# Instance norm over rows of 4096: batch-norm statistics on VectorE for three rows of a tile, two ScalarE passes for the fourth, both engines normalising

## The chip, the cores and the metric

One core of a Trainium2 chip. The metric is the device time of one execution in microseconds (us). The kernel before takes 4961.82 us (median of 4 runs, 4961.57 to 4962.37).

## The reference

```python
x = np.random.randn(256, 256, 4096).astype(np.float32)      # eps = 1e-5
mean = np.mean(x, axis=2, keepdims=True)
var = np.var(x, axis=2, keepdims=True)
out = ((x - mean) / np.sqrt(var + eps)).astype(np.float32)
```

That is 65,536 independent rows of 4096 float32 numbers: 1.07 GB in and 1.07 GB out. The chip's engines that matter here are VectorE (DVE in the profiles) and ScalarE (ACT), which compute, SyncE (SP), which issues the transfers, and 16 DMA engines, which carry them out. Engines wait for each other through semaphores, counters that an instruction or a transfer increments. A transfer has landed when each of the 16 DMA engines has incremented its semaphore.

## The kernel before

The rows go through 128 tiles of 128 partitions x 4 rows (8.39 MB each) in three buffers. One queue on SyncE issues everything in a fixed order, store t and then load t+2:

```python
def store(s, t):
    take(S, done[s], K + 1)              # all rows of the tile are normalised
    S.dma_start(out=rows_of(out_t, t), in_=X[s][:, :, :]).then_inc(stored[s], 16)

def load(s, t, wait=True):
    if wait:
        take(S, stored[s], 16)           # the buffer's last store has landed
    S.dma_start(out=X[s][:, :, :], in_=rows_of(x_t, t)).then_inc(loaded[s], 16)
# ...
with S.Fori(0, rounds) as i:
    for t in range(L0, L0 + BUFS):
        store(t % BUFS, (t, BUFS, rounds, i))
        load((t + 2) % BUFS, (t + 2, BUFS, rounds, i))
```

Per tile VectorE takes the sum of each row in a pass that writes the row back and accumulates, ScalarE takes the sum of squared deviations, and VectorE normalises, except for three quarters of the last row, which ScalarE does:

```python
for r in range(r0, r0 + k):
    V.tensor_scalar(out=x[:, r, :], in0=x[:, r, :], scalar1=1.0 / d, scalar2=None, op0=ALU.mult, op1=ALU.add,
                    accum_out=mean[s][:, r : r + 1]).then_inc(means, 1)
# ... ScalarE, row by row:
A.activation(out=junk, in_=x[:, r, :], func=AF.Square, bias=mean[s][:, c], scale=-float(d), accum_out=ss[s][:, c])
# ... VectorE: reciprocal, bias product, and
V.tensor_scalar(out=x[:, r, f], in0=x[:, r, f], scalar1=rstd[s][:, c], scalar2=nbias[s][:, c],
                op0=ALU.mult, op1=ALU.add).then_inc(dn, 1)
```

The first and the last tile go in halves of two rows. The whole kernel:

## Time and profile before

| | before |
|---|---|
| time, median | 4961.82 us |
| busy VectorE, ScalarE | 66%, 49% |
| busy DMA engines | 9 tenths or more in every slice, 433 GB/s |
| period of a tile | 38.64 us in most of the run |
| landing of a load to issue of the tile's store | 26.2 us |

Read it from the DMA side: 2147.5 MB have to pass, and the engines that pass them are never idle. What SyncE's queue waits for (line, who waits for whom: us in total, times, longest) doesn't contradict that:

```profile
SPq L68 <- DVE x L112: 4757.1, 130, 38.3
SPq L68 <- DMA out_dram<-x: 47.7, 3, 30.7
```

SyncE waits for VectorE nearly all the time, but SyncE only issues transfers. Those that it has issued before are still under way meanwhile. The prediction shows the lines that tell it.

### The profile page before, as it was taken

How to read it: one execution, taken by the hardware profiler on the slowest of the kernel's cores; microseconds unless marked ns; L12 is line 12 of the kernel's file. 1: busy time of each engine (PE TensorE's matmuls, PEld its weight loads, DVE VectorE, ACT ScalarE, POOL GpSimd, SP SyncE). 2: the span in 40 equal slices, each digit the busy share in tenths (PEclk: the TensorE clock that was granted, in tenths of full speed). 3: DMA queues.
4: the chain of work that ended last, by engine and by line, in shares of the span. 5: the costliest groups of instructions: out<-in, count | busy, mean ns of one | idle time of the engine just before them, and what ended most of it. 6: DMA issues, size and time to landing. Idle time of an engine off the chain costs nothing.

```text
span 4960.2 us, 5938 instructions
## 1 busy us (share of the span) xinstructions
DVE 3298.0 (66%) x2049; ACT 2407.7 (49%) x1412; POOL 0.2 (0%) x4
## 2 busy tenths in 40 slices
DVE  6666666666666666666666666666666666666666
ACT  4455444554445544455445544455444554445544
POOL 0000000000000000000000000000000000000000
DMA  9999999999999999999999999999999999999999
GB/s 422 431 435 433 431 435 433 432 437 432 432 438 432 433 437 432 433 437 432 435 435 432 436 434 431 438 433 431 438 433 432 438 432 433 438 432 433 438 432 405
DMA packets 37298, 2147.52 MB, mean 433 GB/s; under 512 B 4144, under 2 KB 4144, under 8 KB 4144
## 3 DMA queue, kind: packets, MB, share of 16 engines
q1 hardware_dynamic: 37296, 2147.50, 100.0%
q14 instruction: 2, 0.02, 0.0%
HBM read 1073.74 MB, written 1073.74 MB: 433 GB/s over the span
## 4 chain that ended last, share of the span: by engine, by line
DVE 62%; another core or an unknown queue 31%; issue 4%; DMA 2%; ACT 0%; DVEq 0%; ACTq 0%; SPq 0%
DVE x L87 44%; DVE x L112 17%; DMA x<-in_x_dram 1%; DVE nbias L100 1%; DMA out_dram<-x 1%; DVE rstd L98 1%; ACT junk L137 0%; DVEq L68 0%; DVEq L219 0%; ACT L146 0%; ACT std L146 0%; ACTq L68 0%; ACTq L67 0%; SPq L265 0%
## 5 line engine op out<-in xcount | busy, mean ns | idle before, releaser
L87 DVE TENSOR_SCALAR_CACHE_REDUCE x<-x 128x4096 f32<-128x4096 f32 x512 | 2232.3, 4416 | 1580.4 <-DMA x<-in_x_dram 1580.4
L137 ACT ACTIVATE junk<-x,mean 128x4096 f32<-128x4096 f32 x512 | 1883.1, 3678 | 2367.2 <-DVE x L87 2367.2
L112 DVE TENSOR_SCALAR x<-x,rstd,nbias 128x4096 f32<-128x4096 f32 (+1 forms) x512 | 1004.2, 2004 | 33.9 <-DVE nbias L100 29.3
L151 ACT ACTIVATE x<-x,nbias,rstd 128x3072 f32<-128x3072 f32 x130 | 383.2, 2948 | 146.2 <-DVEq L68 146.2
L137 ACT ACTIVATION_READ_ACCUMULATOR junk<-x,mean 128x1 f32 x512 | 95.5, 187 | 0.0
L146 ACT ACTIVATE std<-ss,eps_tile 128x2 f32<-128x2 f32 x256 | 75.6, 295 | 19.1
L98 DVE RECIPROCAL rstd<-std 128x2 f32<-128x2 f32 x256 | 40.7, 159 | 19.4 <-ACT std L146 19.4
L100 DVE SCALAR_TENSOR_TENSOR nbias<-mean,rstd 128x2 f32<-128x2 f32 x256 | 41.1, 161 | 8.9
L87 DVE DVE_READ_ACCUMULATOR x<-x 128x1 f32 x512 | 42.3, 83 | 0.0
L137 ACT ACT_TABLE_LOAD x1 | 1.3, 1283 | 1.2 <-DVE eps_tile L216 1.2
L146 ACT ACT_TABLE_LOAD x1 | 1.3, 1283 | 0.1
L216 DVE MEMSET eps_tile<- 128x1 f32 x1 | 0.1, 59 | 1.0 <-SPq L192 1.0
L251 POOL MEMSET const-bfloat16-1.0<- 128x1 bf16 x1 | 0.1, 101 | 0.0
L251 POOL MEMSET const-uint8-127<- 128x1 uint8 x1 | 0.1, 101 | 0.0
L251 POOL MEMSET const-float32-1.0<- 128x1 f32 x1 | 0.1, 99 | 0.0
L251 POOL MEMSET const-float32-0.0<- 128x1 f32 x1 | 0.1, 98 | 0.2 <-issue 0.2
## 6 DMA issues: line engine op xcount, KB each, us to landing
out_dram<-x SPq DMA_DIRECT2D x4, 4096.0 KB, 19.6
x<-in_x_dram SPq DMA_DIRECT2D x2, 4096.0 KB, 16.7
x<-in_x_dram SPq DMA_DIRECT2D x127, 50.3
out_dram<-x SPq DMA_DIRECT2D x126, 31.5
```

The costliest lines, as they stand in the source:

```text
L87: V.tensor_scalar(out=x[:, r, :], in0=x[:, r, :], scalar1=1.0 / d, scalar2=None, op0=ALU.mult, op1=ALU.add, accum_out=mean[s][:, r : r + 1 ...
L98: mine(V.reciprocal(out=rstd[s][:, c], in_=std[s][:, c]))
L100: mine(V.scalar_tensor_tensor(out=nbias[s][:, c], in0=mean[s][:, c], scalar=-1.0 / d, in1=rstd[s][:, c], op0=ALU.mult, op1=ALU.mult))
L112: V.tensor_scalar(out=x[:, r, f], in0=x[:, r, f], scalar1=rstd[s][:, c], scalar2=nbias[s][:, c], op0=ALU.mult, op1=ALU.add,).then_inc(dn, 1)
L137: mine(A.activation(out=junk, in_=x[:, r, :], func=AF.Square, bias=mean[s][:, c], scale=-float(d), accum_out=ss[s][:, c]))
L146: A.activation(out=std[s][:, c], in_=ss[s][:, c], func=AF.Sqrt, bias=eps_tile, scale=1.0 / d**3).then_inc(stds, 1)
L151: A.activation(out=x[:, last, :Q], in_=x[:, last, :Q], func=AF.Identity, bias=nbias[s][:, c], scale=rstd[s][:, c]).then_inc(dn, 1)
L216: V.memset(eps_tile, eps / d**2).then_inc(ready, 1)
L251: nc = _bacc.Bacc("TRN2", target_bir_lowering=False, num_devices=1)
```

## The change

The intent is to take work off VectorE. Row 0 of a tile gets its mean and its variance from two ScalarE passes; rows 1 to 3 get theirs from the batch-norm instructions, which give both in one reading pass without writing the row; ScalarE normalises rows 0 and 1 and part of row 3, VectorE row 2 and the rest. Cut to its core:

```diff
-    Q = 3072
+    Q = 2752
+    F = 512
...
-        for r in range(r0, r0 + k):
-            V.tensor_scalar(out=x[:, r, :], in0=x[:, r, :], scalar1=1.0 / d, ..., accum_out=mean[s][:, r : r + 1],
-            ).then_inc(means, 1)
+        for r in range(r0 + 1, r0 + k):
+            for j in range(d // F):
+                mine(V.bn_stats(out=stats[s][:, r, j, :], in_=x[:, r, j * F : (j + 1) * F]))
+                if j == 4 and (r - r0) % 2 == 0:
+                    scales(r - 2)
+            V.wait_ge(own_v, own)
+            V.bn_aggr(out=mv[s][:, r, :], in_=stats[s][:, r]).then_inc(means, 1)
...
-        for r in range(r0, last + 1):        # ScalarE: squares of all rows
+        A.activation(out=junk, in_=x[:, r0, :], func=AF.Identity, scale=1.0 / d, accum_out=mv[s][:, c, 0])
+        A.activation(out=junk, in_=x[:, r0, :], func=AF.Square, bias=mv[s][:, c, 0], scale=-1.0, accum_out=ss[s][:, c])
...
+            for r, f in [(b + 1, slice(0, Q))] if final else [(b, slice(0, d)), (b + 1, slice(0, d))]:
+                A.activation(out=x[:, r, f], in_=x[:, r, f], func=AF.Identity, bias=nbias[...], scale=rstd[...])
```

`mine` gives each statistics instruction an increment of a semaphore. SyncE's part is the same.

More of the change, by code (lines that the diff above doesn't have):

```diff
@@ L30 @@
     n, d = x_flat.shape
-    assert n % (P * K) == 0 and d & (d - 1) == 0
+    assert n % (P * K) == 0 and d % F == 0
     ntiles = n // (P * K)
@@ L47 @@
     X = [pool.tile([P, K, d], fp32, name=f"x{s}") for s in range(BUFS)]
-    mean, ss, std, rstd, nbias = (
-        [pool.tile([P, K], fp32, name=f"{name}{s}") for s in range(BUFS)]
-        for name in ("mean", "ss", "std", "rstd", "nbias")
+    stats = [pool.tile([P, K, d // F, 6], fp32, name=f"stats{s}") for s in range(BUFS)]
+    mv = [pool.tile([P, K, 2], fp32, name=f"mv{s}") for s in range(BUFS)]
+    ss, std, rstd, nbias = (
+        [pool.tile([P, K], fp32, name=f"{name}{s}") for s in range(BUFS)] for name in ("ss", "std", "rstd", "nbias")
     )
@@ L57 @@
     stored = [nc.alloc_semaphore(f"stored{s}") for s in range(BUFS + 1)]
+    landed = nc.alloc_semaphore("landed")
+    own_a = nc.alloc_semaphore("own_a")
     own_v = nc.alloc_semaphore("own_v")
-    own_a = nc.alloc_semaphore("own_a")
     means = nc.alloc_semaphore("means")
@@ L82, in mine, with scales @@
             return instruction.then_inc(own_v, 1)
-        if ld:
-            take(V, ld, 16)
-        for r in range(r0, r0 + k):
-            V.tensor_scalar(
-                out=x[:, r, :], in0=x[:, r, :], scalar1=1.0 / d, scalar2=None, op0=ALU.mult, op1=ALU.add,
-                accum_out=mean[s][:, r : r + 1],
-            ).then_inc(means, 1)
-        for b in range(r0, r0 + k, 2):
-            c = slice(b, b + 2)
-            final = b == r0 + k - 2
-            if final:
-                take(V, stds, (b - r0) // 2 + 1)
-            else:
-                V.wait_ge(stds, (b - r0) // 2 + 1)
+        def scales(b, final=False):
+            c = slice(b, b + 2)
+            wait = take if final else (lambda engine, sem, count: engine.wait_ge(sem, count))
+            wait(V, stds, (b - r0) // 2 + 2)
             mine(V.reciprocal(out=rstd[s][:, c], in_=std[s][:, c]))
@@ L100, in vector_tile @@
             mine(V.scalar_tensor_tensor(
-                out=nbias[s][:, c], in0=mean[s][:, c], scalar=-1.0 / d, in1=rstd[s][:, c], op0=ALU.mult, op1=ALU.mult
+                out=nbias[s][:, c], in0=mv[s][:, c, 0], scalar=-1.0, in1=rstd[s][:, c], op0=ALU.mult, op1=ALU.mult
             ))
-            if final:
-                take(V, own_v, own)
-            else:
-                V.wait_ge(own_v, own)
-            if final:
-                V.sem_inc(scaled, 1)
-            for r in range(b, b + 2):
-                c = slice(r, r + 1)
-                f = slice(Q, d) if r == r0 + k - 1 else slice(0, d)
-                V.tensor_scalar(
-                    out=x[:, r, f], in0=x[:, r, f], scalar1=rstd[s][:, c], scalar2=nbias[s][:, c],
-                    op0=ALU.mult, op1=ALU.add,
-                ).then_inc(dn, 1)
+            wait(V, own_v, own)
+            V.sem_inc(scaled, 1)
+        if ld:
+            take(V, ld, 16)
+        V.sem_inc(landed, 1)
+        for r in range(r0 + 1, r0 + k):
[5 more added lines that the diff above has]
+            V.bn_aggr(out=mv[s][:, r, :], in_=stats[s][:, r]).then_inc(means, 1)
+        scales(r0 + k - 2, final=True)
+        for r in (r0 + k - 2, r0 + k - 1):
+            c = slice(r, r + 1)
+            f = slice(Q, d) if r == r0 + k - 1 else slice(0, d)
+            V.tensor_scalar(
+                out=x[:, r, f], in0=x[:, r, f], scalar1=rstd[s][:, c], scalar2=nbias[s][:, c],
+                op0=ALU.mult, op1=ALU.add,
+            ).then_inc(dn, 1)
     def scalar_tile(s, r0=0, k=K, ld=None, dn=None):
@@ L120, in scalar_tile @@
         dn = done[s] if dn is None else dn
-        last = r0 + k - 1
-        own = 0
-        def mine(instruction):
-            nonlocal own
-            own += 1
-            return instruction.then_inc(own_a, 1)
-        for r in range(r0, last + 1):
-            c = slice(r, r + 1)
-            if own:
-                A.wait_ge(own_a, own)
-            if r == last:
-                take(A, means, k)
-            else:
-                A.wait_ge(means, r - r0 + 1)
-            mine(A.activation(
-                out=junk, in_=x[:, r, :], func=AF.Square, bias=mean[s][:, c], scale=-float(d), accum_out=ss[s][:, c]
-            ))
-            if (r - r0) % 2:
-                c = slice(r - 1, r + 1)
-                if r == last:
-                    take(A, own_a, own)
-                else:
-                    A.wait_ge(own_a, own)
-                A.activation(
-                    out=std[s][:, c], in_=ss[s][:, c], func=AF.Sqrt, bias=eps_tile, scale=1.0 / d**3
-                ).then_inc(stds, 1)
@@ L149, in scalar_tile @@
-        c = slice(last, last + 1)
-        take(A, scaled, 1)
-        A.activation(
-            out=x[:, last, :Q], in_=x[:, last, :Q], func=AF.Identity, bias=nbias[s][:, c], scale=rstd[s][:, c]
-        ).then_inc(dn, 1)
+        c = slice(r0, r0 + 1)
+        take(A, landed, 1)
+        A.activation(
+            out=junk, in_=x[:, r0, :], func=AF.Identity, scale=1.0 / d, accum_out=mv[s][:, c, 0]
+        ).then_inc(own_a, 1)
+        A.wait_ge(own_a, 1)
+        A.activation(
+            out=junk, in_=x[:, r0, :], func=AF.Square, bias=mv[s][:, c, 0], scale=-1.0, accum_out=ss[s][:, c]
+        ).then_inc(own_a, 1)
@@ new lines, in scalar_tile @@
+        take(A, own_a, 2)
+        A.activation(
+            out=std[s][:, c], in_=ss[s][:, c], func=AF.Sqrt, bias=eps_tile, scale=1.0 / d
+        ).then_inc(stds, 1)
+        for b in range(r0, r0 + k, 2):
+            final = b == r0 + k - 2
+            if final:
+                take(A, means, k - 1)
+            else:
+                A.wait_ge(means, b - r0 + 1)
+            c = slice(max(b, r0 + 1), b + 2)
+            A.activation(
+                out=std[s][:, c], in_=mv[s][:, c, 1], func=AF.Sqrt, bias=eps_tile, scale=1.0
+            ).then_inc(stds, 1)
+            take(A, scaled, 1)
+            for r, f in [(b + 1, slice(0, Q))] if final else [(b, slice(0, d)), (b + 1, slice(0, d))]:
+                c = slice(r, r + 1)
+                A.activation(
+                    out=x[:, r, f], in_=x[:, r, f], func=AF.Identity, bias=nbias[s][:, c], scale=rstd[s][:, c]
+                ).then_inc(dn, 1)
@@ L214 @@
             take(S, stored[s], 16)
-        V.memset(eps_tile, eps / d**2).then_inc(ready, 1)
+        V.memset(eps_tile, eps).then_inc(ready, 1)
         halves(vector_tile, 0, True)
```

## The prediction

> **What bounds the kernel now.** I read the views in this order: busy shares and slices of the page, the DMA queue, one tile in the timeline, the issue rows, and only then the chain that ended last, because here the chain alone misleads.
>
> From the page of the kernel before:
>
> ```profile
> span 4960.2 us, 5938 instructions
> DVE 3298.0 (66%) x2049; ACT 2407.7 (49%) x1412; POOL 0.2 (0%) x4
> DMA  9999999999999999999999999999999999999999
> GB/s 422 431 435 433 431 435 433 432 437 432 432 438 432 433 437 432 433 437 432 435 435 432 436 434 431 438 433 431 438 433 432 438 432 433 438 432 433 438 432 405
> q1 hardware_dynamic: 37296, 2147.50, 100.0%
> ```
>
> VectorE is at two thirds and ScalarE at half in every slice, so neither fills its time. The DMA row is 9 in all 40 slices, and packets of the one queue take 100.0% of the 16 engines' span. Each input byte is read once and each output byte written once: 2147.5 MB in 4960.2 us are 433 GB/s.
>
> One tile in the timeline, from one store to the next (start, duration, engine, line, operation):
>
> ```profile
> 2009.40 0.34 SPq L165 DMA_DIRECT2D out_dram<-x  x1
> 2009.98 0.35 SPq L170 DMA_DIRECT2D x<-in_x_dram  x1
> 2021.72 4.42 DVE L87 TENSOR_SCALAR_CACHE_REDUCE x<-x 128x4096 f32<-128x4096 f32 x1 [12.53 <-DMA x<-in_x_dram]
> ...
> 2044.66 3.14 DVE L112 TENSOR_SCALAR x<-x,rstd,nbias 128x4096 f32<-128x4096 f32 x2 [0.19 <-DVE nbias L100]
> ...
> 2047.95 0.34 SPq L165 DMA_DIRECT2D out_dram<-x  x1
> 2048.53 0.35 SPq L170 DMA_DIRECT2D x<-in_x_dram  x1
> 2060.39 4.42 DVE L87 TENSOR_SCALAR_CACHE_REDUCE x<-x 128x4096 f32<-128x4096 f32 x1 [12.59 <-DMA x<-in_x_dram]
> ```
>
> Tiles land at 2021.72 and 2060.39: a period of 38.67 us. Compute takes 26.2 us of it (landing at 2021.72 to the store's issue at 2047.95). Then both engines idle 12.5 us for the next load. A tile is 8.39 MB in and 8.39 MB out, 16.78 MB; over 38.67 us that is 434 GB/s, the rate of the whole page. So nothing in the period is left over for a stall of the queue.
>
> The issue rows show the same from the queue's side:
>
> ```profile
> x<-in_x_dram SPq DMA_DIRECT2D x127, 50.3
> out_dram<-x SPq DMA_DIRECT2D x126, 31.5
> ```
>
> Half the period, 19.3 us, is one transfer. When store t is issued at 2009.40, load t+1 has some 12 us to go (it lands at 2021.7). The store then lands after 12 + 19.3 = 31.3 us, and the load behind it after 12 + 19.3 + 19.3 = 50.6 us. That matches 31.5 and 50.3: transfers stand in line behind a queue that never empties. The store could come up to about 12 us later without a gap in that queue, and coming earlier wins it only a longer time in line.
>
> Now the chain:
>
> ```profile
> DVE 62%; another core or an unknown queue 31%; issue 4%; DMA 2%; ACT 0%; DVEq 0%; ACTq 0%; SPq 0%
> ```
>
> It charges 62% to VectorE, since it steps from each load's issue back to the VectorE instruction that released the store ahead of it. It doesn't see that the transfer stood in line after its release. The 31% of "unknown queue" is roughly the 12.5 us wait in each 38.7 us period. I let the slices and the landing times decide: the bound is the DMA engines.
>
> **What the Trainium skill says.** "DMA: Bandwidth & Descriptors", section "Bandwidth", under "Where 436 GB/s comes from", gives a fabric ceiling of 435.2 GB/s for the 16 ports. The trace agrees: 435 GB/s over 2021.70 to 2041.00 and 432 to 437 over neighbouring stretches. An estimate from that page: 2147.5 MB at 435.2 GB/s need 4934.5 us, so at most 26 us (0.5%) separate this kernel from the ceiling, start and end latency included. "HBM Reference"[...] says that a core streaming alone goes above its share of the memory, to about 425 GB/s; the trace shows slightly more, 433. "SBUF — State Buffer", section "SBUF: two separate sides", says that engine accesses and DMA don't contend. The trace agrees within its resolution: 437 GB/s over 2009.40 to 2021.70 with both engines idle, and 435 over the next 19.3 us with VectorE busy throughout. "VectorE: DVE Perf Modes", section "The perf-mode tier table", gives float32 tensor_scalar twice the single rate and reductions the single rate. The trace agrees: normalising 4096 elements takes 2411 ns, the pass with an accumulator 4416 ns. No section gives a time for the batch-norm instructions.
>
> **The change part by part.** The durations come from these groups, kept apart by shape (count | total us, mean ns):
>
> ```profile
> L87 DVE TENSOR_SCALAR_CACHE_REDUCE x<-x 128x4096 f32<-128x4096 f32 x512 | 2232.3, 4416 | 1580.4 <-DMA x<-in_x_dram 1580.4
> L137 ACT ACTIVATE junk<-x,mean 128x4096 f32<-128x4096 f32 x512 | 1883.1, 3678 | 2367.2 <-DVE x L87 2367.2
> L112 DVE TENSOR_SCALAR x<-x,rstd,nbias 128x4096 f32<-128x4096 f32 x382 | 910.3, 2411 | 33.9 <-DVE nbias L100 29.3
> L151 ACT ACTIVATE x<-x,nbias,rstd 128x3072 f32<-128x3072 f32 x130 | 383.2, 2948 | 146.2 <-DVEq L68 146.2
> L112 DVE TENSOR_SCALAR x<-x,rstd,nbias 128x1024 f32<-128x1024 f32 x130 | 104.9, 807 | 0.0
> ```
>
> Removed from VectorE per tile: four mean passes at 4.42 us, 17.7 us, with their accumulator reads (4 x 0.08), and two of three full normalisations (2 x 2.41). Added: 24 batch-norm statistics of 512 elements and three aggregations. I size the statistics from the mean pass, which also goes at one element per step: successive passes start 4.35 us apart, 1.06 ns per element; an eighth of that is 0.54 us, and I allow 0.07 us more for the fixed part of an instruction (the two-element operations take 0.16 us). That is 0.61 us each, 14.6 us in all; the aggregations, 48 inputs each, get 0.25 us each with their wait, 0.8 us. What stays: reciprocal and bias product twice (4 x 0.16), one full row at 2.41 us, and 1344 elements of the last row, interpolated between 807 ns at 1024 and 2411 at 4096: 0.97 us. Sum: 14.6 + 0.8 + 0.6 + 3.4 = 19.4 us a tile, 2480 us in all, near 50% where it had 66%.
>
> ScalarE loses four squares (4 x (3.68 + 0.19)) and keeps two passes of that size, 7.7 us. It has three small square roots instead of two, 0.9 us. It gains two full normalisations: 2948 ns for 3072 elements, scaled by the slope between its forms (its squares give at most 3678/4096 = 0.9 ns per element), makes about 3.8 us for 4096 and 2.7 us for 2752. Sum: 7.7 + 0.9 + 7.6 + 2.7 = 18.9 us, 2420 us in all, about 49% as before. Identity, square and root should share one table: before, the table was loaded twice in the whole run (1.28 us each), and I expect no load per tile.
>
> Latency of one tile, from landing: ScalarE's two passes and roots end at about 8.8 us; VectorE has by then done row 1 (8 x 0.61 + 0.35 = 5.2 us) and five pieces of row 2 (8.3 us), so it waits about half a microsecond for the roots, spends 0.6 us on the scales and releases ScalarE at 9.4 us. ScalarE normalises rows 0 and 1 until 17.1 us; VectorE finishes rows 2 and 3 near 16.8. Root, scales and the last normalisations take 0.4 + 0.7 + 3.3 us: done at about 21.5 us, against 26.2. The store is issued 4.7 us earlier, and the queue's backlog at that moment grows from 12.5 to about 17 us. All of the gain lies beside the transfers; on the path that sets the end it is worth 0.
>
> Ends: the DMA engines are the limit there too. In the kernel before the first store half is issued at 31.54 us, while load 1 still occupies the queue to about 41; the last one at 4941.7, while the store ahead of it has work to about 4949. Both come earlier by some 5 to 8 us after the change and wait that much longer. I give the ends 0 us, with 2 or 3 us of doubt either way for engines among the 16 that run ahead of others.
>
> Predicted: 4961.5 us.
>
> **The rivals.** First, compute counts: if the chain's 62% were right, 4.7 us less per tile would bring 128 x 4.7 = 600 us, so 4360 us. It would need 493 GB/s, above anything sustained in this trace; the 12.5 us idle in each period speak against it as well. Second, the batch-norm instruction is far slower than one element per step: with the other VectorE work near 4.8 us and ScalarE hidden, it becomes the bound once 24 of them exceed 38.7 - 4.8 = 33.9 us, or 1.41 us each, 2.3 times my size. At 1.5 us each the period would be near 41 us and the time about 5240 us. Nothing in the trace shows the instruction, so this can't be excluded, but even double its size stays hidden. Third, the handshakes between the two engines or a table load per use: two loads per tile would add 2.6 us and the chain would end near 24 us, still below 38.7, so 4961 us. Fourth, less engine traffic lets the DMA go faster: the 437 against 435 above would be 0.5% at the very most, and the stretches differ as much by load and store phase; a time of 4945 us would be its upper hope.
>
> **Range and chances.** The three runs before lie within 0.6 us, and every rival I believe in leaves the queue full. I take 4956 to 4966 us, mostly for small differences at the ends and in how loads and stores interleave. Faster by over 2% needs the DMA above its ceiling: 0.01. Slower by over 2% needs the second rival: 0.02. Within 2%: 0.97.
>
> **What would show it.** Right: DMA row 9 throughout and 433 GB/s; period of landings near 38.67 us; VectorE near 50%; store issued about 21 to 22 us after landing; time from issue to landing up by the 4.7 us of earlier issue, from 31.5 to about 36 us for stores and from 50.3 to about 55 for loads; VectorE idle before its tile's first statistics up from 12.5 to about 17 us. Wrong: any gap in the DMA slices, statistics of over 1.4 us, a table load in every tile, or a period that follows the compute.

## The result

The changed kernel takes 4981.48 us (median of 4 runs, 4978.88 to 4984.67), 19.7 us more than before. The ratio is 1.004 with a 95% interval of 1.0022 to 1.0057; it is the mean time of one kernel's runs over that of the other's of the same rounds, so not quite the ratio of the medians. It is slower, clear of noise, and outside the predicted range of 4956 to 4966 us.

The page of the changed kernel, the lines that answer to those shown of before:

```profile
span 4982.9 us, 7979 instructions
DVE 2480.7 (50%) x4211; ACT 2368.6 (48%) x1290; POOL 0.2 (0%) x4
DMA  9999999999999999999999999999999999999998
GB/s 421 435 430 437 432 431 437 430 436 433 435 435 433 435 431 437 434 433 435 432 436 433 435 434 430 429 435 430 429 429 429 430 433 430 430 429 430 429 433 384
q1 hardware_dynamic: 37296, 2147.50, 99.9%
x<-in_x_dram SPq DMA_DIRECT2D x127, 56.3
out_dram<-x SPq DMA_DIRECT2D x126, 37.5
```

VectorE fell from 66% to 50%, as worked out. The DMA row is still all nines but for the last slice. But its rate goes down in the course of the run, from about 434 to 430 GB/s in the last sixteen slices (the very last apart, in which the run ends): the queue is never empty and yet slower. Transfers stand in line longer (37.5 us from issue to landing of a store, 31.5 before), as stores come earlier.

The groups by shape, for the sizes that the prediction estimated (count | total us, mean ns):

```profile
L103 DVE BATCH_NORM_STATS2 stats<-x 128x6 f32<-128x512 f32 x3056 | 1846.8, 674 | 2332.9 <-DMA x<-in_x_dram 2314.4
L147 ACT ACTIVATE x<-x,nbias,rstd 128x4096 f32<-128x4096 f32 x252 | 944.1, 3793 | 71.9 <-DVEq L96 71.9
L147 ACT ACTIVATE x<-x,nbias,rstd 128x2752 f32<-128x2752 f32 x130 | 348.5, 2681 | 92.7 <-DVEq L70 92.7
L112 DVE TENSOR_SCALAR x<-x,rstd,nbias 128x1344 f32<-128x1344 f32 x130 | 126.7, 975 | 0.0
L107 DVE BATCH_NORM_AGGREGATE mv<-stats 128x2 f32<-128x48 f32 x382 | 142.0, 372 | 13.2
```

None of these is on the path. A tile's first statistics begin when its load has landed, so their starts give the period. From the timeline, three stretches of the run:

```profile
940.20 4.85 DVE L103 BATCH_NORM_STATS2 stats<-x 128x6 f32<-128x512 f32 x8 [18.90 <-DMA x<-in_x_dram]
978.87 4.85 DVE L103 BATCH_NORM_STATS2 stats<-x 128x6 f32<-128x512 f32 x8 [18.18 <-DMA x<-in_x_dram]
...
2025.06 4.85 DVE L103 BATCH_NORM_STATS2 stats<-x 128x6 f32<-128x512 f32 x8 [18.32 <-DMA x<-in_x_dram]
...
2045.71 0.34 SPq L161 DMA_DIRECT2D out_dram<-x  x1
2046.29 0.35 SPq L166 DMA_DIRECT2D x<-in_x_dram  x1
...
2063.89 4.85 DVE L103 BATCH_NORM_STATS2 stats<-x 128x6 f32<-128x512 f32 x8 [18.33 <-DMA x<-in_x_dram]
...
4047.23 4.84 DVE L103 BATCH_NORM_STATS2 stats<-x 128x6 f32<-128x512 f32 x8 [18.60 <-DMA x<-in_x_dram]
4086.12 4.85 DVE L103 BATCH_NORM_STATS2 stats<-x 128x6 f32<-128x512 f32 x8 [18.39 <-DMA x<-in_x_dram]
```

The period is 38.67 us near 940, 38.83 near 2025, 38.89 near 4047. The store is issued 20.65 us after the landing (2025.06 to 2045.71), when the load under way has 18.2 us to go. Nothing waits for compute: VectorE idles 18 us ahead of every tile.

**Where the 22.7 us between the two profiled spans arise.** The trace holds the time of each of the 16 semaphore increments by which a transfer reports its landing, one from each DMA engine. Counting tiles from 0, the last increment of the same load came at (us):

```
tile     before    changed   difference   period before / changed since the line above
 32      1248.8     1249.2       0.4
 72      2794.3     2801.4       7.1      38.64 / 38.81
120      4649.3     4670.3      21.0      38.65 / 38.94
```

Until tile 32 both are equal. From about 1400 us on the changed kernel's period is 38.82 to 38.83 us, and from about 3100 us it is near 38.95 us. So the loss has two stages, of 0.19 and of 0.31 us per tile.

**The 16 engines one by one.** The same increments say how far the first engine is ahead of the last. Before, this lead grows to 7.5 us by 1250 us and stays there until about 4490 us. In the changed kernel it is 8.0 us at 1400 us, then grows by 0.19 us per tile, to 16.2 us near 3100 us, and stays about there. Growth means that the last engine is slower than the first; that it is one engine alone, the packets show. The trace also has a start and a duration for each DMA packet: each transfer is, on each engine, eight packets of 64 KB and a small one that reports the landing. It doesn't name the engine, but each packet starts 3 or 4 ns before the one ahead of it ends, so that the packets can be strung together, engine by engine. An undisturbed 64 KB packet takes 2418 ns. Beyond that, in ns, for two successive transfers (a store, the load behind it) near 2370 us of the changed kernel:

```
                       store: excess of its 8 packets       load: excess of its 8 packets
last engine            14 14 14 47 14 23 14 28              0 0 3 1 1 1 8 1
15th engine             0  0  0  0  0  0  0  0              0 0 0 0 0 0 0 0
first engine            0  0  0  0  0  0  0  0              0 0 0 0 0 0 0 0
```

One engine of 16 loses 168 ns on each store and 15 ns on each load, 0.18 us per tile; the others lose nothing. A load counts as landed when its last engine is through, so this one engine sets the pace. Averages over 16 engines hide it. In the kernel before there is such an engine too, with 0.03 to 0.07 us on each store; it was not the last until about 4490 us, and from then to the end the period was 38.72 us.

The 38.64 us of the kernel before are no accident either: an undisturbed engine starts its 64 KB packets 2.414 us apart, and the 16 of a load and a store take 38.62 us, to which the two small packets come.

### The profile page after: what moved, and what is told of

Same layout as the page of the kernel before. It is cut to its first block, busy times and chain, and to the rows that moved or that the text cites. A ratio compares the mean times of both kernels' runs of the same rounds, so it can differ in the third digit from the quotient of the medians.

```text
span 4982.9 us, 7979 instructions
## 1 busy us (share of the span) xinstructions
DVE 2480.7 (50%) x4211; ACT 2368.6 (48%) x1290; POOL 0.2 (0%) x4
## 4 chain that ended last, share of the span: by engine, by line
another core or an unknown queue 45%; ACT 40%; DVE 9%; issue 3%; DMA 1%; DVEq 1%; ACTq 0%; SPq 0%
ACT x L147 19%; ACT junk L127 10%; ACT junk L123 10%; DVE x L112 7%; ACT std L141 1%; DMA x<-in_x_dram 1%; DVE nbias L92 1%; DVE rstd L90 1%; ACT std L131 1%; DVEq L70 0%; ACTq L70 0%; DVEq L96 0%; DVE stats L103 0%; DVEq L215 0%
## 5 line engine op out<-in xcount | busy, mean ns | idle before, releaser
L103 DVE BATCH_NORM_STATS2 stats<-x 128x6 f32<-128x512 f32 x3056 | 1846.8, 674 | 2332.9 <-DMA x<-in_x_dram 2314.4
L123 ACT ACTIVATE junk<-x 128x4096 f32<-128x4096 f32 x130 | 466.4, 3587 | 2381.2 <-DVEq L70 2381.2
L147 ACT ACTIVATE x<-x,nbias,rstd 128x4096 f32<-128x4096 f32 (+1 forms) x382 | 1292.6, 3415 | 164.6 <-DVEq L70 92.7
L127 ACT ACTIVATE junk<-x,mv 128x4096 f32<-128x4096 f32 x130 | 478.1, 3678 | 4.2
L112 DVE TENSOR_SCALAR x<-x,rstd,nbias 128x4096 f32<-128x4096 f32 (+1 forms) x260 | 429.3, 1693 | 24.3 <-DVE nbias L92 24.3
L107 DVE BATCH_NORM_AGGREGATE mv<-stats 128x2 f32<-128x48 f32 x382 | 142.0, 372 | 13.2
L141 ACT ACTIVATE std<-mv,eps_tile 128x1 f32<-128x1 f32 (+1 forms) x256 | 73.4, 287 | 0.0
L92 DVE SCALAR_TENSOR_TENSOR nbias<-mv,rstd 128x2 f32<-128x2 f32 x256 | 41.2, 161 | 8.7
L131 ACT ACTIVATE std<-ss,eps_tile 128x1 f32<-128x1 f32 x130 | 38.2, 294 | 15.0
L127 ACT ACTIVATION_READ_ACCUMULATOR junk<-x,mv 128x1 f32 x130 | 24.3, 187 | 0.0
## 6 DMA issues: line engine op xcount, KB each, us to landing
x<-in_x_dram SPq DMA_DIRECT2D x127, 56.3
out_dram<-x SPq DMA_DIRECT2D x126, 37.5
```

The source lines that it names most:

```text
L92: mine(V.scalar_tensor_tensor(out=nbias[s][:, c], in0=mv[s][:, c, 0], scalar=-1.0, in1=rstd[s][:, c], op0=ALU.mult, op1=ALU.mult))
L103: mine(V.bn_stats(out=stats[s][:, r, j, :], in_=x[:, r, j * F : (j + 1) * F]))
L107: V.bn_aggr(out=mv[s][:, r, :], in_=stats[s][:, r]).then_inc(means, 1)
L123: A.activation(out=junk, in_=x[:, r0, :], func=AF.Identity, scale=1.0 / d, accum_out=mv[s][:, c, 0]).then_inc(own_a, 1)
L127: A.activation(out=junk, in_=x[:, r0, :], func=AF.Square, bias=mv[s][:, c, 0], scale=-1.0, accum_out=ss[s][:, c]).then_inc(own_a, 1)
L131: A.activation(out=std[s][:, c], in_=ss[s][:, c], func=AF.Sqrt, bias=eps_tile, scale=1.0 / d).then_inc(stds, 1)
```

## The experiments

Two theories at first. LEAD: earlier stores let the fast engines run further ahead, until they run dry, start together, and disturb one another. For it spoke that from 3100 us on, where the lead stops growing, packets of the other engines become longer too. COUNT: the engine that loses time loses it to something that the compute engines emit per instruction; per tile the changed kernel has 43 instructions on them (4211 + 1290 in 128 tiles) where the kernel before has 27. Every kernel was run four times (run 11 five times), beside the kernel before on the same chip, whose medians then were 4962.1 to 4962.6 us.

**1. The changed kernel with late stores.** One more VectorE pass in each tile, result unchanged:

```diff
+        r = r0 + k - 1
+        mine(V.tensor_scalar(out=x[:, r, :], in0=x[:, r, :], scalar1=1.0, scalar2=None,
+                             op0=ALU.mult, op1=ALU.add, accum_out=spare))
         scales(r0 + k - 2, final=True)
```

> The changed kernel with one long VectorE pass (4.4 us) put in before the last scales, so that each store is issued about 26 us after landing, as in the kernel before; only two instruction records per tile are added. Theory LEAD (stores issued earlier let the fast DMA engines run up to 16 us ahead of the slowest, where they run dry and start together, and their packets stall): the lead is capped near 11 to 12 us, the stalls go, time 4960 to 4966 us. Theory COUNT (one of the 16 DMA engines loses 14 to 56 ns on packets of its stores in proportion to the number of instructions that the compute engines issue meanwhile, and this engine sets the landings): the instruction count is that of the changed kernel, so 4978 us or more, period 38.8 us or longer once the slow engine is last.

Measured: 4985.57 us (4977.67 to 4987.27), ratio 1.0044 (1.0027 to 1.0061). In its trace the lead stopped at 12 to 13 us, as LEAD says, but the period had gone to 38.81 us at 1250 us and to 39.0 near 3500. The stores came 24.3 us after landing (2022.79 to 2047.08) and not 26, so two thirds of the earlier issue were undone (20.65 in the changed kernel, 26.2 before), and that saved nothing. Against LEAD as the start of the loss, runs 2 and 3 say more.

**2. The kernel before with 24 tiny instructions per tile.**

```diff
             take(V, ld, 16)
+        for j in range(6 * k):
+            mine(V.memset(spare[:, j : j + 1], 0.0))
```

> The kernel before with 24 tiny VectorE memsets (128x1, each with a semaphore increment) at the start of each tile: 51 instead of 27 compute instructions per tile, store issued only about 1.5 us later. Theory LEAD: the store is later, not earlier, so 4962 us as before. Theory COUNT: more instructions than the changed kernel's 43, so one DMA engine's stores lose 0.2 us or more per tile, the period goes to 38.8 us early in the run, time 4975 to 4985 us.

Measured: 4982.71 us (4979.23 to 4985.19), ratio 1.0039 (1.0022 to 1.0056), with a period of 38.81 us from about 1700 us on and near 39.0 later. No batch-norm instruction is needed: 24 memsets of one element per partition slow the old kernel as much as the change does. Its stores are issued 27.0 us after landing (2021.79 to 2048.81), later than in the kernel before without the memsets, so LEAD can't explain this run.

**3 and 4. A kernel with hardly any compute ("thin"), without and with tiny instructions.** VectorE only makes out = 2x + 1, ScalarE nothing (wrong result):

```diff
+        for j in range(10 * k):                                  # run 4 only
+            mine(V.memset(spare[:, j : j + 1], 0.0))
+        if own:
+            take(V, own_v, own)
+        for r in range(r0, r0 + k):
+            V.tensor_scalar(out=x[:, r, :], in0=x[:, r, :], scalar1=2.0, scalar2=1.0,
+                            op0=ALU.mult, op1=ALU.add).then_inc(dn, 2 if r == r0 else 1)
```

> Wrong result on purpose (out = 2x + 1): four VectorE passes of 2.4 us per tile, nothing on ScalarE, store issued about 10 us after landing, 4 compute instructions per tile. Theory LEAD: stores come even earlier than in the changed kernel (backlog 29 us), so the stalls are at least as large: 4978 us or more. Theory COUNT: hardly any instructions, no slow engine: 4955 to 4962 us.

> The thin kernel (wrong result on purpose) with 40 tiny memsets with semaphore increments per tile ahead of its four passes: 44 compute instructions per tile, store issued about 13 us after landing. Theory LEAD: as the thin kernel without them. Theory COUNT: slower than the thin kernel by 10 to 25 us, one engine's packets lengthened by 14 to 56 ns.

Measured: 4961.40 us (4959.93 to 4963.26) without, 4978.45 us (4978.23 to 4979.61) with the memsets. Early stores alone cost nothing, against LEAD; 40 memsets per tile cost 17 us. From the pages, run 3 and then run 4:

```profile
span 4958.2 us, 1872 instructions
GB/s 422 431 435 432 431 434 433 435 434 432 436 434 432 435 436 432 435 436 432 434 436 433 434 436 432 434 436 432 433 436 434 433 435 435 433 435 435 433 435 413
```

```profile
span 4976.7 us, 7122 instructions
GB/s 421 433 434 435 431 434 435 434 434 434 435 434 434 434 434 434 434 436 432 435 436 432 436 432 436 432 435 432 436 432 435 433 435 434 434 435 434 434 435 349
```

The rows differ hardly, except in the last slice. In run 4, 15 engines keep their pace and one falls behind by 0.18 us per tile, to 17 us at the end; the others are done and it isn't, hence 349 GB/s. And the run shows when the time is lost, since its memsets are one short burst at the start of a tile. Of the packets of 16 engines under way during the burst, one is longer by 155 ns (median over the tiles after 1000 us; 137 in the lowest tenth, 164 in the highest) and the next longest by 0.

**5. The changed kernel with fewer statistics instructions**, one per row in place of eight (wrong result):

```diff
-            for j in range(d // F):
+            for j in range(1):
```

> The changed kernel with one batch-norm statistics instruction of 512 elements per row in place of eight (wrong result on purpose: statistics of an eighth of each row): 22 instead of 43 compute instructions per tile, everything else of the change kept, stores still issued about 20 us after landing. Theory COUNT: 4960 to 4965 us, the slow engine's loss below 0.1 us per tile. If something else of the change (both engines normalising, ScalarE's two passes, early stores) costs the time: 4975 us or more.

Measured: 4967.07 us (4966.67 to 4967.29), ratio 1.0009 (0.9993 to 1.0026). It is a little above what I expected, since the slow engine still loses 0.12 us per tile, not under 0.1; but it was the last one only from about 2500 us on. About three quarters of the 19.7 us go with 21 tiny instructions per tile, while the two passes on ScalarE, the early stores and the normalising on both engines are all still there.

**6 to 8. What of an instruction counts?** The thin kernel with 40 memsets of which only the last increments a semaphore; with 80 memsets with increments; with 40 increments by VectorE's sequencer and no instruction on the engine:

```diff
+        for j in range(10 * k - 1):                              # run 6
+            V.memset(spare[:, j : j + 1], 0.0)
+        mine(V.memset(spare[:, 63:64], 0.0))

+        for j in range(20 * k):                                  # run 7
+            mine(V.memset(spare[:, j : j + 1], 0.0))

+        for j in range(10 * k):                                  # run 8
+            own += 1
+            V.sem_inc(own_v, 1)
```

> The thin kernel with 40 tiny memsets per tile of which only the last increments a semaphore. If the cost goes with the instruction: 4975 to 4980 us, as with 40 increments. If it goes with the semaphore update: 4960 to 4963 us, as without the memsets.

> The thin kernel with 80 tiny memsets with increments per tile instead of 40. Theory COUNT with a cost in proportion (40 cost 0.18 us per tile): 0.36 us per tile on the slow engine, period about 39.0 us once it is last, time 4990 to 5005 us. If the loss saturates: 4978 us.

> The thin kernel with 40 increments of a semaphore per tile done by VectorE's sequencer alone, without an instruction on the engine itself. If instructions of the sequencer count like the engine's: about 4978 us. If only instructions that run on the engine count: 4960 to 4963 us.

Measured: 4972.37 us (4971.75 to 4973.67), 5059.01 us (5058.16 to 5059.99; ratio 1.0195, 1.0178 to 1.0212, "unclear" by the 2% rule) and 4977.95 us (4977.70 to 4978.43). Run 6 lies between both expectations: one packet is longer by 108 ns where it was 155 with increments. So both the instruction and its semaphore update count, 2.7 ns for a memset alone (108 / 40) and 3.9 with its increment (155 / 40). Run 8 costs as much as run 4 without any instruction on the engine. Run 7 was expected at 4990 to 5005. Its first part is as expected, 288 ns per burst (213 on one packet, 75 on the next) and a period of 38.96 us; but at 3000 us its lead reaches 27 us, which is where its fast engines run out of issued work, and from there the period is 40.3 us. That looks like the second stage of the changed kernel at larger scale.

**9 and 10. The changed kernel again, and with fewer increments.** In run 10 only the last of each row's eight statistics instructions increments the semaphore; the result is correct:

```diff
-                mine(V.bn_stats(out=stats[s][:, r, j, :], in_=x[:, r, j * F : (j + 1) * F]))
+                stat = V.bn_stats(out=stats[s][:, r, j, :], in_=x[:, r, j * F : (j + 1) * F])
+                if j == d // F - 1:
+                    mine(stat)
```

> The changed kernel as it is, again, for comparison on the same chip: 4978 to 4985 us, one DMA engine's stores longer by some 0.16 us, its lag behind the others growing by 0.19 us per tile once it is last.

> The changed kernel, correct, with a semaphore increment only on the last of each row's eight statistics instructions: 21 of some 89 semaphore updates per tile gone, instructions unchanged. Theory COUNT (each instruction and each semaphore update costs one DMA engine some ns): the loss falls from 0.19 to about 0.15 us per tile, time 4968 to 4977 us. If the increments don't matter: 4978 to 4985 us.

Measured: 4980.44 us (4978.06 to 4983.71) and 4974.99 us (4973.44 to 4978.48). The period with the slow engine last is 38.80 us in run 10, against 38.82 to 38.83 in run 9: a loss of 0.16 instead of 0.19 us per tile over the 38.64. Fewer updates help, by about the expected size (0.15 us expected). The times of the two kernels just touch (4978.06 the lowest of run 9, 4978.48 the highest of run 10), so it is the period that shows it. The packets agree: while the slow engine is last, its stores lose 162 ns in run 9 and 142 in run 10 (means between 2500 and 3450 us), about 1 ns for each of the 21 increments taken out.

**11 and 12. The same burst at another moment.** The slow engine loses on its stores. Is that because it stores while compute runs? Its store begins when its load lands, which starts the tile's compute, and takes 19.3 us. In run 11 the burst comes after 27 us, behind two passes per row; in run 12 after some 22 us, behind three writes of a PSUM tile:

```diff
             ).then_inc(dn, 2 if r == r0 else 1)
+        for j in range(3):                                       # run 12
+            mine(V.memset(junk, 0.0))
+            V.wait_ge(own_v, own)
+        for j in range(10 * k):
+            mine(V.memset(spare[:, j : j + 1], 0.0))
+        take(V, own_v, own)
```

> A thin kernel (wrong result on purpose) with two VectorE passes per row, about 28 us per tile, and the 40 tiny memsets with increments after them, when the slowest DMA engine is in the middle of its next load. If the loss falls on whatever packet is under way while the events happen: some 150 ns on one or two middle packets of its loads, its stores nearly free of it, time 4972 to 4982 us. If only stores suffer: no loss, 4958 to 4963 us.

> The thin kernel (wrong result on purpose, store issued about 10 us after landing) with its 40 tiny memsets with increments moved from the start of the tile to some 22 us after landing, behind three long writes of a PSUM tile that only pass the time: by then the slowest DMA engine has gone over from its store to its load. The run with the burst after 27 us was 4962 us in its timed runs, so now: if only stores suffer, no packet under the burst is longer, period 38.64 us throughout, 4958 to 4963 us. If the burst costs wherever it falls: one packet longer by about 150 ns per tile as with the burst at the start, 4975 to 4980 us.

Measured: run 11 4962.06 us (four timed runs 4961.24 to 4963.15), run 12 4961.33 us (4960.50 to 4962.12). COUNT as I had it missed both: the same 40 instructions cost nothing here. The timelines of run 4 and run 12, one tile each:

```profile
2024.01 1.16 DVE L88 MEMSET spare<- 128x1 f32 x40 [28.62 <-DMA x<-in_x_dram]
2025.31 8.90 DVE L92 TENSOR_SCALAR x<-x 128x4096 f32<-128x4096 f32 x4
2034.36 0.34 SPq L144 DMA_DIRECT2D out_dram<-x  x1
2043.55 0.35 SPq L149 DMA_DIRECT2D x<-in_x_dram  x1
```

```profile
2020.81 8.90 DVE L88 TENSOR_SCALAR x<-x 128x4096 f32<-128x4096 f32 x4 [15.60 <-DMA x<-in_x_dram]
2029.86 0.34 SPq L146 DMA_DIRECT2D out_dram<-x  x1
...
2039.36 3.47 DVE L92 MEMSET junk<- 128x4096 f32 x1 [0.93 <-DVE junk L92]
2040.22 0.35 SPq L151 DMA_DIRECT2D x<-in_x_dram  x1
2042.90 0.93 DVE L95 MEMSET spare<- 128x1 f32 x40
```

In run 4 the burst lies right behind the landing at 2024.01, while the last engine stores; in run 12 it lies 22.1 us behind it (2020.81 to 2042.90), while that engine loads. In run 12's trace the longest packet under the burst has an excess of 1 ns in the median, and the period is 38.64 us from 940 us to the end. So what counts are events that fall into the store of that engine.

Runs 11 and 12 differ from run 4 in more than the moment, since other work goes ahead of the burst. But the trace of run 1 says the same within one kernel, as its compute outlasts the slow engine's store. Means over its 35 tiles between 1500 and 2900 us: the first load packet of that engine has 8 instructions of the compute engines (their sequencers' included) in its time and an excess of 1 ns; six of the eight store packets have 4 to 7 of them and an excess of 10 to 25 ns, and the one that has 12 an excess of 38 ns.

One run of 11, the profiled one, took 5008.74 us, 0.9% above the other four. Its trace shows stalls of up to about 1 us on last packets of stores and loads of most engines, of a kind that its other timed runs can't have had in this number. I draw nothing from it and can't explain it.

**What stays open.** By which path an instruction or an increment reaches that engine's packets is not settled. The small writes that such events could cause are one candidate, among them those of a recorder of events. No run shows such writes. Every run here lists a recorded span, so a run without any recording was not to be had, and I can't say whether the 20 us would be there without it. Which of the 16 engines is the slow one, and whether it is the same one in every run, the traces don't tell. Fetching of instructions is not it as far as the trace shows: its queue moved 4 packets in the whole changed kernel, and run 8 without engine instructions costs the same. Why the pace gets worse once the lead has reached the queue's depth (0.3 us per tile in place of 0.19) was seen in four kernels and not taken apart. It is no small part: by an estimate from the periods (0.12 us more per tile over the last 46 tiles) some 5 of the 22.7 us.

No version beats the kernel before. The thin kernel, with next to no instructions, takes the same 4961 us, so these runs leave nothing for a change of the compute to win.

## Why the prediction was wrong

- *The bound*: right. The DMA engines are the limit, and the chain's 62% for VectorE misled. Taking 5.6 us off each tile's compute (26.2 to 20.65 us) won nothing.
- *The sizes*: right. VectorE 2480.7 us for 2480, statistics starting 0.61 us apart (eight in 4.85 us), no table load per tile, ScalarE 2369 us for 2420, store 20.65 us after landing for 21.5. The aggregation was 0.37 us for 0.25, hidden. That VectorE's total is met to 1 us is partly luck: the statistics took 1846.8 us for about 1870, the aggregations 142.0 for about 100, and these errors cancel.
- *First rival* (compute counts, 4360 us) and *second* (statistics over 1.4 us, 5240 us): rightly dropped. *Third* (handshakes and table loads): none seen.
- *The step that failed*: "All of the gain lies beside the transfers; on the path that sets the end it is worth 0", and with it "every rival I believe in leaves the queue full". The queue was full and the transfers were slower all the same. The term for what compute does to the DMA engines was put at 0; it measured +19.7 us. The mechanism missing is that instructions and semaphore updates of the compute engines lengthen the store packets of one DMA engine of 16, 0.18 us per tile here, and a transfer is as late as its last engine.
- *Fourth rival*: it looked at the right place with the wrong sign and the wrong measure. I compared 437 GB/s with engines idle to 435 with VectorE busy, took that for the resolution of the trace, and thought of bytes. What counts is the number of instructions and increments, and a loss of 0.5% on one engine doesn't show in a mean over 16. The single transfers did show it: the period of the kernel before was 38.72 us in its last ten tiles, and I had averaged over it.
- *The range*: 4956 to 4966 us, mostly for the ends. The ends were right (from the last load's landing to the end of the span 59.2 us before, 59.3 after), the middle was not.
- *What would show it*: the "period of landings near 38.67 us" was the sign that failed; issue to landing went up as said (37.5 us for 36, 56.3 for 55).
- *A slip in a source*: what the prediction takes from "HBM Reference" on a core that streams alone stands in that page's section "Specifications (TRN2)"; the prediction named another section.

## What to carry to other kernels

In a kernel like this one, bound by DMA with a queue that never empties, the period is that of the slowest of the 16 engines (38.82 us here, where 15 of them would have kept 38.64): look at the spread of the 16 landings and its growth, not at GB/s. Instructions and semaphore increments are not free there although every engine is half idle; if you have the choice, prefer few large instructions and one increment for a group, or let them run when the slowest engine loads rather than stores. A change that takes busy time off engines that already wait should be judged by its count of instructions too.

## What the Trainium skill lacked or had wrong

- "SBUF — State Buffer", section "SBUF: two separate sides", says that a DMA cannot be slowed by a compute op. For the ports that may hold (run 8 lost as much with no instruction on the engine), but the sentence is read as more: here 40 memsets of one element per partition made one store packet 155 ns longer (2418 ns undisturbed), and 24 per tile made the kernel before 20 us slower.
- "DMA: Bandwidth & Descriptors", section "Bandwidth", lacks how far the 16 engines drift apart under one queue that never empties: 7.5 us in the kernel before, 16 us in the changed one, 27 us in run 7.
- No page tells what an instruction or a semaphore update costs a DMA engine: 2.7 ns for a memset, 3.9 ns with its increment, if it falls into a store of that one engine, and nothing that the runs show if it falls into a load.
- "VectorE: DVE Perf Modes", section "The perf-mode tier table", has no row for the batch-norm instructions: 674 ns for statistics of 512 float32 elements (0.61 us from start to start), 372 ns for aggregating eight of them.
